# S5 output products of an encoder layer: chunk columns as the stationary operand, two groups side by side, and a transpose behind them

## The chip, the core and the metric

The kernel runs on one core of a Trainium2 chip, as one launch. The metric is the device time of one execution in microseconds (us). Engines are named as in the profile: PE is TensorE's matmul, PEld its weight load, DVE VectorE, ACT ScalarE, POOL GpSimd, SP SyncE, which issues most of the DMAs.

## The reference

One layer of an encoder on 512 tokens of width 1024 in float32: an S5 state-space mixer and a gated MLP mixer in parallel, merged by gates, then cross-attention to 256 memory tokens and a SwiGLU network of width 2816. The change lies in the S5 branch:

```python
def s5_branch(xa, lam_re, lam_im, log_step, b_re, b_im, c_re, c_im, d, w_glu):
    u = xa.reshape(bsz, seq, 32, 16).transpose(1, 0, 2, 3)       # 32 groups of 16 channels
    y = d.reshape(32, 16) * u
    for direction, reverse in ((0, False), (1, True)):
        y = y + s5_scan(u, ..., reverse)      # 64 complex states a group: h_t = lam h_(t-1) + B u_t; y_t = Re(C h_t)
    y = gelu(y.transpose(1, 0, 2, 3).reshape(bsz, seq, 512))
    return y * sigmoid(y @ w_glu)
```

The result is multiplied by `w_proj_a`, gated, and added to the other mixer's.

## The kernel before

Most of the time goes into large products with weights streamed from HBM in blocks of 512 KB. Each float32 operand is split into a rounded part and a rest (`split`: a cast on ACT, line 85, and a subtraction on DVE, line 86; `whi` and `wlo` for weights), and three matmuls make one product (`mm3`; `product`, line 1103, for the blocks that follow the Strassen pattern with seven block products). `next_w` hands out the split weight blocks and keeps loads and splits running ahead.

The S5 branch runs beside these products as a generator, `s5_program`. `tick(us)` is called after each block of matmuls; it advances a planned clock, in units of 5.2 us, runs what `later(n, fn)` has put off by n units, and lets the generator go on. The order that results is the program order; the framework then schedules the instructions of each engine by a simulated time line, and `in_order` (`keep_in_program_order`) holds marked instructions in program order. Each engine runs its own list in order.

The 512 positions are cut into 64 chunks of 8 (`NCH` = 64, `Q` = 8), the 32 groups into four octets (`NO` = 4, `GO` = 8 groups). For octet `o`:

- `s5_kernels(o)` builds `e0` and `e1` (how a chunk's start state reaches its 8 outputs) on DVE, then in `products` the short convolution kernel `pk`, with 32-column strips of the array at `tile_position=(0, 32 * j)`. `store` copies it into `ks`, a tile with the tag `y`. That tag has one buffer, shared with the results. `spill` writes `ks` to HBM (`kd`), `load` reads it back as the Toeplitz matrices `tt` (one buffer, on POOL's queue for octets 0 and 1, on SP's for 2 and 3).
- `s5_inputs(o)` makes each chunk's input to the states, `s5_scan` carries the states over the chunks on DVE (`zh`).
- `s5_outputs(o)` copies the states at the chunk starts into `ss` (two buffers, lines 918 and 919), and `mix_` multiplies: for each group three matmuls with a 128-column weight (`tt`, `e0`, `e1`) and 64 moving columns (`u`, `ss`), so `py` has (position in chunk, channel) on its 128 partitions and (group, chunk) along the rows. `emit` applies gelu into `y` and stores it with eight DMAs, alternately on SP and POOL, to `yd[o]` in HBM.

Octets 0 and 1 have their kernels built early; those of 2 and 3 are built after the outputs of 0 and 1. All this stands beside the end of the gate products (`gb_evac`, line 1140, a sigmoid) and the products with `w_proj_b` (banks `bx`, `bq`, `qv`; `kept`, line 1130, copies a bank into `u`). When they are done, `ygt` reads `yd` back (line 1224), and the product with `w_glu` follows.

Of the kernel before, what the change touches and what calls it, by code (L numbers as in the profile page):

```python
# [9 lines left out]
F32 = mybir.dt.float32  # L10
F32R = mybir.dt.float32r
AF = mybir.ActivationFunctionType
# [5 lines left out]
P = 128  # L18
# [9 lines left out]
C = 16  # L28
# [11 lines left out]
Q = 8  # L40
NCH = T // Q
NO = 4
GO = G // NO
# [9 lines left out]
def hybrid_layer_kernel(  # L53
# [8 lines left out]
    nc = tc.nc  # L62
# [14 lines left out]
    def bank(name):  # L77
        return pm.tile([P, 512], F32, tag="mm", name=name)

    def aux(name, shape=(P, 512)):  # L80
        return pa.tile(list(shape), F32, tag="aux", name=name)
# [11 lines left out]
    in_order = tc.keep_in_program_order  # L93
# [349 lines left out]
    def later(n, fn):  # L443

        side["later"].append((side["now"] + n, fn))
# [30 lines left out]
    ident = cp.tile([P, P], F32, name="ident")  # L476
# [25 lines left out]
    def row_sums(src):  # L502
        ss = np_.tile([P, 2], F32, tag="ss", name="ss", bufs=2)
        for i in range(2):
            sum_sq(ss[:, i:i + 1], src[:, HALF[i]])
        return ss
# [31 lines left out]
    def slot(tag, shape, dt, name, place=NEAR):  # L538
        n = math.prod(shape[1:])
        t = sp.tile([P, KD * T + ROOM[tag]], dt, tag=tag, name=name)[:, place[tag]:place[tag] + n]  # L540
        return t.rearrange("p (a b c) -> p a b c", a=shape[1], b=shape[2]) if len(shape) == 4 else (
            t.rearrange("p (a b) -> p a b", a=shape[1]))
# [6 lines left out]
    s5p = s5.enter_context(tc.tile_pool(name="s5", bufs=1))  # L549
# [47 lines left out]
    ss = row_sums(xt[:, 1, :])  # L597
    for t in range(1, NT):
        rms_scale(xt[:, t, :], g_mix, xt[:, t, :], ss)
        if t == 1:  # L600
            ss = row_sums(xt[:, 2, :])
# [4 lines left out]
        if t == 2:  # L606
            ss = ss3
# [7 lines left out]
    yd = [dp.tile([GO * C, Q, NCH], F32, name=f"yd{o}") for o in range(NO)]  # L615
# [159 lines left out]
    def lc(t, g):  # L775
        return t[:, g].rearrange("p a b -> p (a b)")
# [129 lines left out]
    def s5_outputs(o):  # L906
        gs = slice(o * GO, (o + 1) * GO)
        while ("oct", o) not in st:
            yield None
        e_re, e_im, tt = st["oct", o]  # L910
        zh, u = st["zh"], st["u"]
        ss = s5p.tile([P, 2, GO, NCH], F32, tag="wt", name="ss", bufs=2)
        ss = (ss[:, 0], ss[:, 1])
        for i, s in enumerate(ss):
            zv = zh[:, :, i, gs].rearrange("p n g -> p g n")
            nc.gpsimd.memset(s[lo_, :, 0:1], 0.0)
            nc.gpsimd.memset(s[hi_, :, NCH - 1:NCH], 0.0)
            nc.scalar.copy(s[lo_, :, 1:NCH], zv[lo_, :, 0:NCH - 1])
            nc.scalar.copy(s[hi_, :, 0:NCH - 1], zv[hi_, :, 0:NCH - 1][:, :, ::-1])

        def mix_():
            ps = aux("py", (P, GO, NCH))
            for g in range(GO):
                nc.tensor.matmul(ps[:, g, :], tt[:, g, :], u[:, o * GO + g, :], start=True, stop=False)
                nc.tensor.matmul(ps[:, g, :], lc(e_re, g), ss[0][:, g, :], start=False, stop=False)
                nc.tensor.matmul(ps[:, g, :], lc(e_im, g), ss[1][:, g, :], start=False, stop=True)
            later(1, lambda: emit(ps))

        def emit(ps):
            y = s5p.tile([P, GO, NCH], F32, tag="y", name="y")  # L930
            nc.scalar.activation(y, ps, AF.Gelu_apprx_tanh)
            ydo = yd[o].rearrange("(g c) l n -> l c g n", c=C)
            for l in range(Q):
                (nc.sync, nc.gpsimd)[l % 2].dma_start(ydo[l], y[C * l:C * l + C])

        later(0.5, mix_)
        yield 0.1

# [48 lines left out]
    u = s5p.tile([P, G, NCH], F32, tag="u", name="u")  # L987
# [74 lines left out]
    for h in range(H):  # L1062
        ps = bank("psv")
# [56 lines left out]
    def unit_bank(name):  # L1120
        return bank(name).rearrange("p (j t) -> p j t", j=2)
# [45 lines left out]
    for q, ts in ((5, T1), (6, T0)):  # L1167
        for i in range(2):
            k = slice(2 * i, 2 * i + 2)
# [95 lines left out]
    h = slot("A", (P, NT, D), F32, "h")  # L1265
# [223 lines left out]
    for t0 in (0, 2):  # L1489
        ps = {t: bank(f"pt{t - t0}") for t in (t0, t0 + 1)}  # L1490
# [21 lines left out]
    def acts(unit, f):  # L1512

        if unit < 4:
            return (a_up, a_lo_)[f][:, 2 * unit:2 * unit + 2, :]
        if not rest:
            rest.append(fp.tile([P, KD, T], F32, tag="full", name="rest", bufs=1))
        return rest[0][:, 2 * f:2 * f + 2, :]
# [36 lines left out]
    def put(u, f, ts, src):  # L1555
        dst = acts(u[1] // 512, f)[:, :, ts]
        if u[0] is w_gate:
            nc.scalar.activation(dst, src, AF.Silu)
        else:
            nc.vector.tensor_tensor(dst, dst, src, ALU.mult)  # L1560
# [7 lines left out]
    ps = [bank("pf0"), bank("pf1")]  # L1568
# [67 lines left out]
    for i, u in enumerate(UNITS):  # L1636
        final = i == len(UNITS) - 1
        x, v = begun
        q = unit_bank("pq")
# [132 lines left out]
    for i in range(2):  # L1772
        p = aux("pcut", (P, 256))
# [37 lines left out]
```

## Time and profile before

| what | value |
|---|---|
| median of three runs | 889.34 us |
| lowest, highest | 888.95, 893.28 us |
| the profiled execution | 889.93 us |
| its span in the profile | 888.2 us |
| granted TensorE clock, mean | 0.996 |
| products `py`, first to last | 247.0 to 306.9 us |
| matmul records of `py` | 192 (three lines of 64) |

The span is what the profile covers, from the first instruction to the last; the profiled execution's own time has 1.7 us more. A matmul of full float32 operands shows up as two records. In a timeline row a bracket tells the engine's idle time before the instruction and what ended it; `x2` at the end counts merged instructions. Rows of the chain of waits give the start, the length, and what the chain ran through.

### The profile page before, as it was taken

To read this page: it belongs to the slowest core of one execution; us is meant where nothing else is said; L and a number is where in the kernel's file an instruction comes from. 1 tells how busy PE (TensorE), PEld (TensorE's weight loads), DVE (VectorE), ACT (ScalarE), POOL (GpSimd) and SP (SyncE) were. 2 spreads that over 40 slices of the span, in tenths; PEclk is the share of its full clock that TensorE was granted. 3 is DMA by queue.
4 is the path that set the end of the run, shared out by engine and by line. 5 is a ranking of instruction groups with operands and counts; after the bars stand their busy time and mean duration, and the time that the engine had idled before them with its cause. 6 is when DMAs were issued, how large, how long until landed. Compare 5 with 4: busy or idle time off the path is not lost.

```text
span 888.2 us, 14796 instructions
## 1 busy us (share of the span) xinstructions
PE 870.7 (98%) x5744; PEld 776.9 (87%) x5744; DVE 643.3 (72%) x1048; ACT 486.2 (55%) x714; POOL 106.8 (12%) x165
## 2 busy tenths in 40 slices
PE   8999999999999999999999999999999999999996
PEld 5788888888888988889899978999999999988875
DVE  6698644899757367659857736776878767899875
ACT  5745975244396253448556625645455454655664
POOL 1005201111032101000001001101120111000010
PEclk9999999999999999999999999999999999999999
DMA  8669367887425699734579736637899998356572
GB/s 255 198 185 227 75 190 168 212 190 190 124 79 155 177 323 233 257 111 148 184 217 253 196 95 189 167 109 170 215 241 225 216 237 228 95 176 214 192 239 93
DMA packets 118408, 165.36 MB, mean 186 GB/s; under 512 B 11825, under 2 KB 84161, under 8 KB 118210
## 3 DMA queue, kind: packets, MB, share of 16 engines
q1 hardware_dynamic: 97474, 135.74, 47.1%
q0 software_dynamic: 20576, 28.15, 20.1%
q8 instruction: 45, 0.74, 0.3%
q10 hardware_dynamic: 288, 0.52, 0.2%
q14 instruction: 25, 0.20, 0.1%
HBM read 157.61 MB, written 46.63 MB: 230 GB/s over the span
## 4 chain that ended last, share of the span: by engine, by line
PE 89%; DMA 3%; DVE 2%; ACT 2%; SPq 2%; issue 1%; POOL 0%; POOLq 0%; DVEq 0%; ACTq 0%
PE pf L358 25%; PE pt L358 17%; PE px L1112 12%; PE pq L1112 6%; PE dx L358 5%; PE dq L358 3%; PE pv L1112 3%; PE qx L1112 2%; PE dv L358 2%; PE pz L873 2%; PE psc L358 1%; PE qq L1112 1%; PE ptr L520 1%; PE po L358 1%; PE bq L1112 1%; DMA slab<-in_s_log_step_dram 1%
## 5 line engine op out<-in xcount | busy, mean ns | idle before, releaser
L86 DVE TENSOR_TENSOR wlo<-wraw,whi 128x1024 fp32r<-128x1024 f32 (+1 forms) x145 | 172.3, 1188 | 92.8 <-ACT whi L85 92.4
L85 ACT CAST whi<-wraw 128x1024 fp32r<-128x1024 f32 (+1 forms) x145 | 148.5, 1025 | 150.6 <-PE pf L358 41.7
L358 PE MATMUL pf<-xn,whi 128*128 128x512 f32 x448 | 139.3, 391 | 0.0
L358 PEld LDWEIGHTS pf<-xn,whi 128*128 128x128 f32 x448 | 83.5, 188 | 16.8
L358 PE MATMUL pf<-xn,wlo 128*128 128x512 f32 x224 | 87.3, 390 | 0.0
L1112 PE MATMUL px<-fn,whi 128*128 128x256 f32 x480 | 83.3, 276 | 0.0
L1112 PEld LDWEIGHTS px<-fn,whi 128*128 128x128 f32 x480 | 72.6, 188 | 0.2
L85 ACT CAST whi<-b 128x1024 fp32r<-128x1024 f32 x40 | 42.2, 1054 | 50.7 <-PE px L1112 27.7
L86 DVE TENSOR_TENSOR wlo<-b,whi 128x1024 fp32r<-128x1024 f32 x40 | 48.9, 1223 | 28.0 <-ACT whi L85 28.0
L1112 PE MATMUL px<-fn,wlo 128*128 128x256 f32 x240 | 66.4, 277 | 0.0
L1112 PE MATMUL pq<-s,whi 128*128 128x256 f32 x320 | 55.0, 276 | 0.0
L358 PE MATMUL dx<-whi,s 128*128 128x512 f32 x170 | 53.4, 391 | 0.4 <-DVE h L1736 0.4
L85 ACT CAST whi<-t 128x1024 fp32r<-128x1024 f32 x30 | 31.6, 1054 | 35.3 <-PE pv L1112 12.4
L86 DVE TENSOR_TENSOR wlo<-t,whi 128x1024 fp32r<-128x1024 f32 x30 | 36.7, 1225 | 19.4 <-ACT whi L85 19.4
L358 PEld LDWEIGHTS pf<-xn,wlo 128*128 128x128 f32 x224 | 42.0, 188 | 8.8
L1112 PEld LDWEIGHTS pq<-s,whi 128*128 128x128 f32 x320 | 48.2, 188 | 0.0
L1112 PEld LDWEIGHTS px<-fn,wlo 128*128 128x128 f32 x240 | 45.1, 188 | 0.0
L358 PE MATMUL pt<-whi,xn 128*128 128x512 f32 x128 | 43.5, 409 | 1.2 <-ACT xn L85 1.2
L1112 PE MATMUL pq<-s,wlo 128*128 128x256 f32 x160 | 44.2, 276 | 0.0
L358 PEld LDWEIGHTS dx<-whi,s 128*128 128x128 f32 x170 | 31.8, 188 | 7.5 <-issue 0.8
L358 PE MATMUL dx<-wlo,s 128*128 128x512 f32 x85 | 33.1, 391 | 0.2 <-DVE wlo L86 0.2
L275 POOL DMA_DIRECT2D dsum<-in_w_down_dram x12 | 13.3, 1109 | 163.3 <-DMA dsum<-in_w_down_dram 163.2
(453 smaller groups left out, 2264.7 us busy)
## 6 DMA issues: line engine op xcount, KB each, us to landing
wraw<-in_w_in_dram SPq DMA_DIRECT2D x36, 512.0 KB, 4.7
dsum<-in_w_down_dram SPq DMA_DIRECT2D x20, 512.0 KB, 5.7
wraw<-dsum SPq DMA_DIRECT2D x20, 512.0 KB, 4.0
b<-in_w_gate_dram SPq DMA_DIRECT2D x15, 512.0 KB, 6.8
b<-in_w_up_dram SPq DMA_DIRECT2D x15, 512.0 KB, 5.1
wraw<-in_w_down_dram SPq DMA_DIRECT2D x15, 512.0 KB, 4.0
dsum<-in_w_down_dram POOLq DMA_DIRECT2D x10, 512.0 KB, 7.4
dsum<-dsum POOLq DMA_DIRECT2D x10, 512.0 KB, 8.3
```

What stands on the lines that cost most here:

```text
L85: hi = nc.scalar.copy(dst_hi, src)
L86: lo = nc.vector.tensor_tensor(dst_lo, src, dst_hi.bitcast(F32), ALU.subtract)
L275: plan[j + step][1].append((0, lambda d=dst, x=more: nc.gpsimd.dma_start(d, x, accum_op=ALU.add)))
L358: m = nc.tensor.matmul(ps, a[x], b[y], start=start and i == 0, stop=stop and i == 2, skip_group_check=free)
L520: nc.tensor.transpose(ps[:, j, :], src[:, k * P:(k + 1) * P], ident)
L873: nc.tensor.matmul(ps[:, g, :], wt[:, g, :], u[:, o * GO + g, :], start=True, stop=True)
L1112: nc.tensor.matmul(ps[:, j, :], a[x], b[y], start=start and j == k == i == 0, stop=k == 3 and i == 2, skip_group_check=True)
```

## The change

`mix_` swaps the operands: the 64 chunk columns of `u` or `ss` are now the weight, and the 128 columns of `tt`, `e0` or `e1` are moving. Two groups, `h` and `4 + h`, are put on two column halves of the array, and their matmuls alternate. `py` so has (group half, chunk) on the partitions and (position, group, channel) along the rows. `emit` only copies it to `y`; a new step `turn_y` transposes it in four full 128 x 128 pieces back to (position half, group, channel) on the partitions, and another new step `put` applies gelu, writes over `y`, and stores it with two DMAs. The steps are half a unit apart. Matmuls and transposes are marked `in_order`, which the former matmuls were not.

```diff
         def mix_():
-            ps = aux("py", (P, GO, NCH))
-            for g in range(GO):
-                nc.tensor.matmul(ps[:, g, :], tt[:, g, :], u[:, o * GO + g, :], start=True, stop=False)
-                nc.tensor.matmul(ps[:, g, :], lc(e_re, g), ss[0][:, g, :], start=False, stop=False)
-                nc.tensor.matmul(ps[:, g, :], lc(e_im, g), ss[1][:, g, :], start=False, stop=True)
+            ps = aux("py", (P, 4, 2, 4, C))
+            for h in range(4):
+                for k in range(3):
+                    for j in range(2):
+                        g = 4 * j + h
+                        a = u[:, o * GO + g, :] if k == 0 else ss[k - 1][:, g, :]
+                        b = (tt[:, g, :], lc(e_re, g), lc(e_im, g))[k]
+                        in_order(nc.tensor.matmul(ps[64 * j:64 * j + 64, :, :, h, :].rearrange("p q d c -> p d q c"), a,
+                                                  b.rearrange("p (d q c) -> p d q c", d=2, q=4),
+                                                  start=k == 0, stop=k == 2, tile_position=(0, 64 * j)))
             later(1, lambda: emit(ps))
 
         def emit(ps):
-            y = s5p.tile([P, GO, NCH], F32, tag="y", name="y")
-            nc.scalar.activation(y, ps, AF.Gelu_apprx_tanh)
-            ydo = yd[o].rearrange("(g c) l n -> l c g n", c=C)
-            for l in range(Q):
-                (nc.sync, nc.gpsimd)[l % 2].dma_start(ydo[l], y[C * l:C * l + C])
+
+            y = s5p.tile([P, 512], F32, tag="y", name="y")
+            nc.scalar.copy(y, ps.rearrange("p q d g c -> p (q d g c)"))
+            later(0.5, lambda: turn_y(y))
+
+        def turn_y(y):
+            ps = aux("pyt", (P, 2, 4, NCH))
+            for q in range(4):
+                in_order(nc.tensor.transpose(ps[:, :, q, :], y[:, q * P:(q + 1) * P], ident))
+            later(0.5, lambda: put(y, ps))
+
+        def put(y, ps):
+            nc.scalar.activation(y, ps.rearrange("p s q n -> p (s q n)"), AF.Gelu_apprx_tanh)
+            ydo = yd[o].rearrange("(s f) (d q) n -> d f s (q n)", s=2, d=2)
+            for d in range(2):
+                (nc.sync, nc.gpsimd)[d].dma_start(ydo[d], y[64 * d:64 * d + 64].rearrange("p (s r) -> p s r", s=2))
```

## The prediction

> **What bounds the kernel now.** The page first: over the whole span TensorE is the limit, and the chain that ended last is mostly its matmuls.
>
> ```profile
> span 888.2 us, 14796 instructions
> PE 870.7 (98%) x5744; PEld 776.9 (87%) x5744; DVE 643.3 (72%) x1048; ACT 486.2 (55%) x714; POOL 106.8 (12%) x165
> PE 89%; DMA 3%; DVE 2%; ACT 2%; SPq 2%; issue 1%; POOL 0%; POOLq 0%; DVEq 0%; ACTq 0%
> ```
>
> Averages hide the stage of the edit, so next I cut its stretch (the four products `py` run between 247 and 307 us) into windows; columns are the window's length and the busy time of PE, PEld, DVE, ACT, POOL.
>
> ```profile
> 244.00:255.00 11.00, 11.00 (x74) 9.93 (x73) 3.46 (x4) 10.69 (x11) 2.19 (x5) 1.00 0.21 71
> 255.00:265.00 10.00, 8.87 (x113) 7.78 (x115) 6.89 (x9) 9.92 (x14) 4.50 (x12) 1.00 0.42 98
> 265.00:280.00 15.00, 14.77 (x150) 14.20 (x140) 13.93 (x17) 11.72 (x16) 3.43 (x11) 1.00 0.43 129
> 280.00:300.00 20.00, 18.87 (x209) 18.54 (x209) 9.92 (x11) 7.64 (x11) 5.78 (x12) 1.00 0.62 170
> ```
>
> So PE is nearly full, but ACT is full with it up to 265 and DVE from 265 to 280. TensorE work taken out here is worth its time only where the other engine gives way too. The timeline of PE shows the waits in it (bracketed: idle before, and what ended it):
>
> ```profile
> 260.62 0.38 PE L1112 MATMUL bq<-s,whi 128*128 128x256 f32 x1 [0.78 <-ACT s L85]
> 261.34 0.38 PE L1112 MATMUL bq<-s,whi 128*128 128x256 f32 x1 [0.34 <-DVE s L86]
> 280.76 0.38 PE L1112 MATMUL bx<-yb_hi,whi 128*128 128x256 f32 x1 [0.99 <-ACT u L1130]
> 301.40 0.41 PE L924 MATMUL py<-u,tt 128*128 128x64 f32 x2 [1.20 <-DMA tt<-kd]
> 306.75 0.48 PE L1112 MATMUL bq<-s,whi 128*128 128x256 f32 x2
> 317.25 2.83 PE bq L1112 x24
> ```
>
> PE waits for ACT, for ACT again, and last for the kernel matrix `tt` of octet 3. The rows at 301.40 and 306.75 also price the old form: 24 matmuls of an octet in 5.35 us. The last row is from the chain of waits: one `product` of 24 matmuls, 2.83 us; from 306.75 to its end at 320.08 the chain holds PE rows alone.
>
> **The change, part by part. TensorE.** Removed: 4 x 5.35 = 21.4 us. Added: 24 matmuls an octet with 64-column weights in two column halves and 128 moving columns, and four transposes. No row shows a 64-column half. The nearest rows are the `pk` matmuls, four 32-column strips with 128 moving columns, issued with the strip as the inner loop as the new ones are, and the transposes `pw`, which use the whole array (from the chain in order of time):
>
> ```profile
> 283.46 0.28 PE L1112 MATMUL bx<-yb_lo,whi 128*128 128x256 f32 x1
> 283.58 0.28 PE L1112 MATMUL bx<-yb_hi,wlo 128*128 128x256 f32 x1
> 283.79 0.42 PE L814 MATMUL pk<-e,bd 128*32 128x128 f32 x8
> 284.03 0.27 PE L819 MATMUL pk<-e,bd 128*16 128x16 f32 x16
> 284.13 0.62 PE L814 MATMUL pk<-e,bd 128*32 128x128 f32 x16
> 284.57 0.28 PE L819 MATMUL pk<-e,bd 128*16 128x16 f32 x16
> 284.78 0.38 PE L1112 MATMUL qv<-yb_hi,whi 128*128 128x256 f32 x1
> 77.97 0.87 PE pw L866 x8
> ```
>
> A matmul has two records. Sixteen strip records take 284.57 - 284.13 = 0.44 us, 0.11 for each set of four side by side; a `pw` record alone takes 0.87 / 8 = 0.109. So a set of 128 moving columns costs 0.11 however many strips share it. Twelve pairs of two records: 24 x 0.11 = 2.64 us if the halves overlap, 48 x 0.11 = 5.28 if they don't. I take 2.64, since four strips overlap. Entering the strips costs 283.79 - 283.58 = 0.21 where the usual step is 0.12, and leaving 0.21 after a set that took 0.10 before: 0.2 together. Four transposes are the `pw` row, 0.87. New sum 2.64 + 0.20 + 0.87 = 3.71, a saving of 1.64 an octet, 6.6 in all, as a ceiling from PE alone. The matmuls alone end 5.35 - 2.84 = 2.5 earlier.
>
> The Trainium skill (TensorEngine Tiling (Array Packing), Key Properties) says that changing the tiling mode drains TensorE, which speaks against eight more changes here. The trace agrees: the 0.2 us just read. By the rule alone the sum has eight more drains without a price; by the row they are 0.8 us, already in it.
>
> **ACT, octet 0.** The removed gelu `L931` and what follows it, on ACT:
>
> ```profile
> 250.46 1.04 ACT L85 CAST whi<-wraw 128x1024 fp32r<-128x1024 f32 x1
> 251.52 1.28 ACT L931 ACT_TABLE_LOAD   x1
> 252.99 0.60 ACT L931 ACTIVATE y<-py 128x512 f32<-128x512 f32 x1 [0.19 <-PE py L926]
> 253.49 1.11 ACT L918 COPY ss<-zh 64x504 f32<-64x504 f32 x1
> ...
> 258.03 1.28 ACT L1140 ACT_TABLE_LOAD   x1
> 259.32 0.60 ACT L1140 ACTIVATE part<-pf 128x512 f32<-128x512 f32 x1
> 259.94 2.18 ACT L85 CAST s<-zf 128x512 fp32r<-128x512 f32 x4
> 260.60 1.29 DVE L86 TENSOR_TENSOR s<-zf,s 128x512 fp32r<-128x512 f32 x2 [3.07 <-ACT s L85]
> ```
>
> The four `ss` copies of octet 2 wait for a buffer that `py` of octet 0 reads, then the table goes back to sigmoid, and only then come the casts `s` for which DVE (3.07 us idle) and PE wait. In the new form `emit` is a plain copy, and the gelu moves behind the last sigmoid in program order (`put` comes one unit, 5.2 us of planned TensorE work, after `emit`, and the sigmoids follow the last feature block). The load at 258.03 goes, and the one at 251.52 moves behind the casts. New order: `py` ends at 252.97 - 2.5 = 250.5, the cast at 251.5, copy 0.6 to 252.1, `ss` 258.03 - 253.49 = 4.54 to 256.6, sigmoid 0.6, first `s` done at 257.8 instead of 260.57: 2.8 earlier. PE gets there at 260.62 - 0.78 - 2.5 + 0.87 (transposes) = 258.2, so the gain at `bq` is 2.3 to 2.8; I take 2.5. The added copy is priced by the `wt` copy, which has its shape:
>
> ```profile
> L867 ACT COPY wt<-pw x16: 561/588/604, 79.0 to 135.8; 128x512 f32<-128x512 f32 x16
> ```
>
> **Octets 1 and 2.** From 265 to 280 DVE is busy 13.93 of 15 us; it begins this queue with the row at 260.60, so it moves forward by the same 2.5 and hardly more. What PE saves on octet 1 it waits for DVE again. A further piece: the 0.99 us before 280.76, where ACT copied `u` late because a table load and the gelu of octet 1 stood ahead. I take 1.0, with bounds 0 and 2. Octet 2 is bound otherwise, by the way of octet 3's kernel matrix:
>
> ```profile
> 285.00 0.38 ACT L829 COPY ks<-pk 128x256 f32<-128x256 f32 x1 [0.52 <-PE pk L819]
> 287.70 6.54 DMA kd<-ks
> 294.37 5.12 SPq L845 DMA_DIRECT2D tt<-kd  x8
> 298.25 2.28 DMA tt<-kd
> ```
>
> Its spill, load and landings are serial from 285.00 to 301.4 and untouched by the edit. The 1.64 of octet 2 ends as a longer wait at 301.40: nothing.
>
> **Octet 3.** After `py` PE runs on without a wait to 320.08, so 1.64 lies on the path.
>
> **Stores.** Eight stores of 32 KB an octet become two of 128 KB; four issues on SP become one, and on POOL too:
>
> ```profile
> 279.32 1.75 SPq L934 DMA_DIRECT2D yd<-y  x4
> 281.11 3.11 SPq L845 DMA_DIRECT2D tt<-kd  x5
> DMA to landing us min/median/max: 1.7/2.1/4.0
> 307.03 0.60 ACT L931 ACTIVATE y<-py 128x512 f32<-128x512 f32 x1 [6.40 <-PE py L926]
> 314.71 1.77 SPq L1224 DMA_DIRECT2D ygt<-yd  x4
> ```
>
> Shorter queues for `tt` of octet 2 (1.75 to about 0.45): octet 2 isn't on the path by the above, so nothing. Larger stores may land from 1.7 to 4.0 us. The last result now passes two more steps, about two products, 5.7 us, with 0.87 of transposes; before, 314.71 - 307.63 = 7.1 us lay between gelu and reload. That cover just holds; I add 0.3, and up to 2.5 if `glu` must wait.
>
> Sum: -2.5 - 1.0 - 0 - 1.64 + 0.3 = -4.8. Against the profiled execution (889.93 us, 1.7 outside its span) 885.1; it lies 0.6 above the median of the three times, 889.34, so I forecast 884.5. The bounds: at best -2.8 - 2.0 - 1.64 - 1.64 (octet 2 counts too) = -8.1, at worst -2.3 - 0 - 1.64 + 2.5 = -1.4; so 881.2 to 887.9.
>
> **Rivals.** (a) PE stays the only bound: all 6.6, and the 1.1 us of waits for `s` go: 881.6. For it: PE 98%; against it: the DVE window. (b) The gain is swallowed: DVE's queue keeps its times, `tt` of octet 3 comes at 301.4 as before, and only octet 3's 1.64 remains: 887.7. For it: the serial chain; against it: DVE's 3.07 us of idle time before `s`. The Trainium skill (TensorEngine Tiling (Array Packing), PSUM Bottleneck) warns of this case: tiling speeds TensorE, not the emptying of PSUM. The ACT windows before 265 agree with it; the copy of 0.6 us that comes in against the 1.28 us load that goes out does not. (c) Slower: the one buffer `y`, shared with `ks`, is held through copy, transposes, gelu and store. Place: `ks` of octet 3 needs it at 285.00. If PE takes the transposes of octet 1 only at 283.6, gelu ends at about 284.6, issue and landing add 2.6, and `ks` is 2.2 late. Then `y` of octet 2, copied when `kd` has landed (294.25), gets its gelu after a product, 294.25 + 0.6 + 2.8 + 0.87 + 0.6 = 299.1; if its store stands on SP ahead of the eight `tt` loads, these start at 299.7 for 294.37, 5.3 late. -4.8 + 1.0 + 2.2 + 5.3 = +3.7: 893.0 (bounds +1.5 to +7). It decides if the store goes ahead of L845. Before, octet 1's store did stand among the `tt` loads, octet 2's behind them. (d) The halves don't overlap, or writing `py` in runs of 16 elements is slow: 5.28 + 0.2 + 0.87 - 5.35 = +1.0 an octet, +4 to +5: 893.8. Against it: the `pk` rows.
>
> **How the numbers follow.** A change of some 0.5% (4.4 us) is about what a measurement of this kernel can tell from no change. Forecast 0.42 (0.26 faster beyond that bound, 0.16 within), (a) 0.18 faster, (b) 0.10 within, (c) 0.20 (half slower, half within), (d) 0.10 slower. Faster 0.44, same 0.36, slower 0.20. The range runs from 880.5, below (a), to 894.0, through (c) and (d); outside lie the far ends of (a), (c) and (d), under 2 in 10. The forecast's own is 881.2 to 887.9.
>
> **What would show it.** Right: 24 new matmuls of an octet from first to last in about 2.7 us; no table load between `ss` copies and the last sigmoids; the first `s` cast near 257; `py` of octet 3 near 298 after a wait of some us. Wrong: that product over 5 us; `ks` waiting for `yd`; SP's store ahead of the last `tt` loads; a wait of several us at `glu`.

## The result, and the profile after

The changed kernel takes 904.67 us (median of 4 runs, 903.75 to 905.06); the kernel before, run beside it, 891.15 us (4 runs, 888.95 to 893.28). The ratio is 1.015, 95% interval 1.0117 to 1.0184: slower by 1.5%, above the forecast (884.5) and above the range (to 894.0). The profiled execution took 905.0 us, of which the page covers 903.2.

The page of the changed kernel, its span, the engines and the chain that ended last by engine:

```profile
span 903.2 us, 14797 instructions
PE 867.9 (96%) x5760; PEld 771.5 (85%) x5760; DVE 643.8 (71%) x1048; ACT 486.0 (54%) x716; POOL 102.2 (11%) x153
PE 88%; DMA 5%; ACT 3%; issue 2%; DVE 1%; SPq 1%; POOLq 0%; POOL 0%; ACTq 0%; DVEq 0%
```

PE has 2.8 us less work (870.7 to 867.9) and the span is 15.0 us longer: PE waits more, and the share of DMA in the chain went from 3% to 5%. The same stretches as before, and one more, from the windows of the changed kernel (columns: length; busy time of PE, PEld, DVE, ACT, POOL; granted clock; DMA share; GB/s):

```profile
255.00:265.00 10.00, 9.66 (x154) 8.62 (x153) 9.77 (x12) 8.27 (x15) 0.74 (x4) 1.00 0.23 69
265.00:280.00 15.00, 8.14 (x61) 7.64 (x61) 13.29 (x16) 11.22 (x13) 2.86 (x9) 0.84 0.43 131
280.00:300.00 20.00, 20.00 (x242) 19.50 (x242) 8.57 (x11) 8.27 (x11) 2.80 (x6) 0.95 0.63 196
318.00:335.00 17.00, 1.50 (x11) 1.30 (x10) 3.09 (x5) 2.13 (x3) 3.19 (x4) 0.65 0.96 271
```

Up to 265 PE is fuller than before (9.66 for 8.87). From 265 to 280 it is busy 8.14 us where it was 14.77, at a clock of 0.84. From 318 to 335 it stands nearly still (1.50 us of work, for 15.78 before). What PE waited for between 244 and 342, from the list of waits (total, times, longest):

```profile
PE pf L358 <- ACT yg_hi L85: 15.5, 1, 15.5
PE bx L1128 <- ACT whi L85: 3.7, 1, 3.7
PE bx L1128 <- ACT u L1146: 3.1, 1, 3.1
PE py L929 <- DMA tt<-kd: 2.2, 1, 2.2
```

Before, no wait of PE in this stretch was above 1.2 us. First the edit itself and the first two waits, on the timeline of PE:

```profile
262.07 0.44 PE L929 MATMUL py<-tt,u 128*64 128x128 f32 x4
264.85 0.66 PE L943 MATMUL pyt<-ident,y 128*128 128x128 f32 x4
265.26 0.48 PE L1128 MATMUL bq<-s,whi 128*128 128x256 f32 x2
275.24 0.58 PE L1128 MATMUL bx<-yb_hi,whi 128*128 128x256 f32 x1 [3.73 <-ACT whi L85]
279.16 0.58 PE L1128 MATMUL bx<-yb_hi,whi 128*128 128x256 f32 x1 [3.12 <-ACT u L1146]
```

Octet 1's 24 matmuls take 264.85 - 262.07 = 2.78 us, for 5.35 before; four transposes take 0.41. The two waits follow. ACT shows what PE waited for:

```profile
257.10 2.19 ACT L85 CAST s<-zf 128x512 fp32r<-128x512 f32 x4
...
272.36 1.28 ACT L947 ACT_TABLE_LOAD   x1
273.66 0.60 ACT L947 ACTIVATE y<-pyt 128x512 f32<-128x512 f32 x1
274.15 1.99 ACT L85 CAST whi<-wraw 128x1024 fp32r<-128x1024 f32 x2
277.30 0.37 ACT L829 COPY ks<-pk 128x256 f32<-128x256 f32 x1 [1.17 <-DMA yd<-y]
278.52 0.59 ACT L1146 COPY u<-bx 128x512 f32<-128x512 f32 x1
287.37 0.59 ACT L937 COPY y<-py 128x512 f32<-128x512 f32 x1
290.97 0.60 ACT L947 ACTIVATE y<-pyt 128x512 f32<-128x512 f32 x1 [1.26 <-PE pyt L943]
295.58 0.37 ACT L829 COPY ks<-pk 128x256 f32<-128x256 f32 x1 [1.06 <-DMA yd<-y]
```

The row at 273.66 is octet 0's gelu; it ran at 252.99 before. `whi` stands behind it and its table load, and ahead of these, from 267.15 to 271.7, behind the four `ss` copies of octet 3. Octet 0 holds the one buffer `y` from its copy at 251.43 until its store lands; `ks` of octet 2 waits for that at 277.30, and `u`, which PE waits for, stands behind it on ACT. Then, once the spill of `ks` has landed, octet 1 may have the buffer: it is copied only at 287.37 though its product was ready at 264.85, its gelu runs at 290.97, and `ks` of octet 3 gets it at 295.58. Before, that copy ran at 285.00. From there the serial chain of spill, load and product moves with it: `py` of octet 3 starts at 310.12 instead of 301.40.

Last, the wait at `glu`. The lists of POOL, first of the kernel before, then of the changed one:

```profile
307.92 2.09 POOL L934 DMA_DIRECT2D yd<-y  x4 [10.13 <-ACT y L931]
...
327.39 1.20 POOL L275 DMA_DIRECT2D qsum<-in_w_q_dram  x1 [14.88 <-DMA qsum<-qsum]
```

```profile
305.27 0.61 POOL L950 DMA_DIRECT2D yd<-y  x1 [6.81 <-ACT y L947]
318.68 1.22 POOL L275 DMA_DIRECT2D qsum<-in_w_q_dram  x1 [12.81 <-DMA qsum<-qsum]
319.35 1.18 POOL L950 DMA_DIRECT2D yd<-y  x1
329.84 0.14 POOL L130 MEMSET pad<- 128x48 f32 x1 [9.31 <-DMA yd<-y]
```

`qsum` is a sum of weight blocks for a later stage: SP copies one block of 512 KB, and POOL adds another to it by an accumulating DMA. It stood 19.5 us behind the last store; now it stands right ahead of it. In program order the store still comes first (experiment 1, which holds the two in that order, has it first); the framework issues the accumulate ahead of it. That it does so because its time line has the last gelu later than before is likely, but not shown. The first copy, on SP, went out earlier too: at 311.11, ahead of the last store, where before it stood at 318.41, behind the reload. The chain of the changed kernel runs through both, and through the reload:

```profile
311.11 6.99 DMA qsum<-qsum
319.35 10.21 DMA yd<-y
330.59 3.12 DMA ygt<-yd
334.58 10.59 PE pf L358 x34
```

SP's half of the last store goes out at 317.40. POOL's half has to wait until the accumulate ahead of it has its copy and is issued; it goes out at 319.35 and lands after 10.21 us. Over all DMAs of `yd` in this kernel the shortest time to landing is 2.5 and the median 3.6 us. So `ygt` is issued at 329.7, and PE, done with the products at about 319.1, starts `glu` at 334.58. Before, it started at 319.91. These 14.7 us are nearly the whole 15.0; up to the end of the products the changed kernel is still 1.0 us ahead (their last matmul starts at 318.81, for 319.79).

### The profile page after: what moved, and what is told of

Its sections match the earlier page's. It is cut to its first block, busy times and chain, and to the rows that moved or that the text cites. A ratio compares the mean times of both kernels' runs of the same rounds, so it can differ in the third digit from the quotient of the medians.

```text
span 903.2 us, 14797 instructions
## 1 busy us (share of the span) xinstructions
PE 867.9 (96%) x5760; PEld 771.5 (85%) x5760; DVE 643.8 (71%) x1048; ACT 486.0 (54%) x716; POOL 102.2 (11%) x153
## 4 chain that ended last, share of the span: by engine, by line
PE 88%; DMA 5%; ACT 3%; issue 2%; DVE 1%; SPq 1%; POOLq 0%; POOL 0%; ACTq 0%; DVEq 0%
PE pf L358 25%; PE pt L358 17%; PE px L1128 12%; PE pq L1128 6%; PE dx L358 5%; PE dq L358 3%; PE pv L1128 3%; PE qx L1128 2%; PE bx L1128 2%; PE dv L358 2%; PE pz L873 2%; DMA yd<-y 1%; PE psc L358 1%; PE qq L1128 1%; PE ptr L520 1%
```

## The experiments

Theory: two things put the last reload late. **(A)** The place on POOL's queue: the last store is issued directly behind the accumulating DMA. **(B)** The buffer `y`, shared with `ks`, is held from the copy to the landing of the store, and everything behind it (`u`, `ks` of octets 2 and 3, `py`, the last gelu) slides. Rivals: the swapped product is itself slow; the late gelu of octet 0 is the harm, not the buffer; the POOL order is harmless. Ratios are to runs of the kernel before on the same chip, beside each group of experiments; they are not quotients of the medians given, and can differ from these by some tenths of a percent.

**1. The order on POOL put back.**

```diff
-            plan[j + step][1].append((0, lambda d=dst, x=more: nc.gpsimd.dma_start(d, x, accum_op=ALU.add)))
+            plan[j + step][1].append((0, lambda d=dst, x=more: onto(d, x)))   # onto: in_order for qsum[4, 0]
...
+            if o == NO - 1:
+                in_order(put_)          # POOL's store of octet 3
```

> The changed kernel, with one order fixed: on POOL's list octet 3's store stands ahead of the accumulating 512 KB DMA (qsum) that was pulled in front of it. Theory 1 (the last store is late because of that DMA): the store lands in about 3.5 us instead of 10.2 and is issued 2 us earlier, ygt is read near 321 instead of 329.7, TensorE's wait at the glu product falls from 15.5 to about 7.5 us; 896.5 us. Rival (the two added steps make the result late by themselves, whatever the queue): the wait stays over 12 us; 902 to 905 us.

Measured: 899.38 us (896.07 to 905.23), ratio 1.0081 (1.0049 to 1.0113); span 897.4. From its chain and its waits:

```profile
318.91 2.92 DMA yd<-y
322.01 5.08 DMA ygt<-yd
```

```profile
PE pf L364 <- ACT yg_hi L85: 7.6, 1, 7.6
```

The store now lands after 2.92 us instead of 10.21 and the wait at `glu` halves, from 15.5 to 7.6. (A) is worth about 5 us here (by the two ratios, 1.015 and 1.0081, about 6), but the kernel is still slower than before: the last gelu itself is late (318.03, for 307.03 before), and the two waits near 275 are untouched (3.9 and 3.1 us).

**2. The results in a buffer of their own.** `y` takes the tag `rb`, a buffer that a tile of the setup (`raw_b`) no longer needs; `ks` keeps the tag `y` to itself.

```diff
-            y = s5p.tile([P, 512], F32, tag="y", name="y")
+            y = s5p.tile([P, 512], F32, tag="rb", name="y")
```

> The changed kernel with a buffer of its own for y (the space of a tile that is dead by then), so that ks no longer waits for y's store; with it the last store comes ahead of the qsum DMA on POOL too. Theory 1 (shared buffer and queue together make the loss): the two waits of TensorE between 271 and 279 us go (6.8 us, and some 2 us at a slow clock), tt of octet 3 comes some 8 us earlier, the wait at glu mostly goes; 886 to 889 us. Rival (lateness of the added steps): the wait at glu stays; 893 to 896 us.

Measured: 885.98 us (885.03 to 887.73), ratio 0.9922 (0.9885 to 0.9959); span 884.3. In the order that results, the store goes ahead of the accumulate by itself (308.64 and 327.44), so this run mends (A) too; against experiment 1, which has (A) mended, the edit differs in the buffer and the marks of order alone, and the medians stand 13.4 us apart. Its waits and, from ACT's timeline, the two `ks` copies:

```profile
PE bx L1128 <- ACT whi L85: 3.9, 1, 3.9
PE pyt L943 <- ACT y L937: 1.9, 1, 1.9
```

```profile
262.91 0.37 ACT L829 COPY ks<-pk 128x256 f32<-128x256 f32 x1
287.14 0.37 ACT L829 COPY ks<-pk 128x256 f32<-128x256 f32 x1 [0.47 <-PE pk L819]
```

`ks` of octet 2 runs 14.4 us earlier than in the changed kernel, that of octet 3 8.4 us, neither waits for `yd`, and the wait at `glu` is gone (its start: 317.38). The wait for `whi` is as long as in experiment 1, so it isn't the buffer's. (B) is shown, and with it that the swap is no loss.

**3. The swapped product alone.** Gelu straight from `py`; the transposes are left out, so the stored result is in another order.

```diff
-            nc.scalar.copy(y, ps.rearrange("p q d g c -> p (q d g c)"))
-            later(0.5, lambda: turn_y(y))
...
+            nc.scalar.activation(y, ps.rearrange("p q d g c -> p (q d g c)"), AF.Gelu_apprx_tanh)
```

> The swapped products and the two larger stores, but gelu straight from the product as before and no transposes (they are left out, so the stored result is in another order). Theory 1 (the swap itself frees TensorE, and the loss comes from the added steps): faster than the old kernel by 5 to 8 us, 882 to 885 us. Rival (what TensorE saves is swallowed by DVE and by the serial way of tt): 888 to 890 us.

Measured: 886.53 us (885.74 to 888.3), ratio 0.9938 (0.9912 to 0.9964). The buffer is still shared, but held for one step only. The rival that the swapped product is slow falls.

**4. The kernel before with its gelu planned later** (`later(2, ...)` for `later(1, ...)` ahead of `emit`).

> The old kernel, with gelu and stores of each octet put off by one more unit, the delay that the added steps bring, and nothing else. Theory 1: y is held longer, but the store still comes ahead of qsum on POOL, so little is lost; 890 to 893 us. Rival (lateness alone is the cost): 897 to 903 us.

Measured: 889.94 us (888.11 to 896.38), ratio 0.9988 (0.9957 to 1.0018). Inconclusive: octet 0's gelu ran at 253.37, as before, since the framework orders each engine by its simulated time line, not by the plan alone. So this run didn't make the gelu late, and says nothing on what a late gelu costs.

**5. The kernel before with the accumulate ahead of the last store.** Plan place 43 for the first copy, and octet 3's POOL stores planned two units later.

```diff
-              [(51 + 2 * i, 2) for i in range(4)] + [(85 + 3 * i, 3) for i in range(3)] +
+              [(43, 3)] + [(51 + 2 * i, 2) for i in range(1, 4)] + [(85 + 3 * i, 3) for i in range(3)] +
```

> The old kernel, with only the order on POOL's list turned round at one place: the accumulating 512 KB DMA (qsum) ahead of POOL's half of octet 3's stores (its SP copy is issued eight weight blocks earlier for that). Theory 1 (a store behind that DMA lands late): POOL's stores of octet 3 land 5 to 10 us later, past the old 314.7 us of the reload, and TensorE waits at the glu product; 893 to 898 us. Rival (the order is harmless, the swap's own lateness did it): 889 to 891 us.

Measured: 897.9 us (897.67 to 906.98), ratio 1.0101 (1.0059 to 1.0143); span 896.1. POOL's timeline and the chain of this run:

```profile
312.47 1.20 POOL L275 DMA_DIRECT2D qsum<-in_w_q_dram  x1 [15.98 <-DMA qsum<-qsum]
313.13 2.65 POOL L944 DMA_DIRECT2D yd<-y  x4
```

```profile
314.70 8.36 DMA yd<-y
323.33 4.16 DMA ygt<-yd
```

With the old product and the old use of the buffer PE waits 9.5 us at `glu`. The place costs twice: POOL, which stands 15.98 us until the accumulate's copy has landed, issues the stores at 313.13 for 307.92 before, and the last of them lands only after 8.36 us. (A) alone makes this kernel 1% slower; nothing of the swap is needed for it.

**6. Two result buffers.** As experiment 2, with two halves of `rb` taken in turn by the octets (`y = st["yy"][:, o % 2]`).

> As with a buffer of its own for y, but two of them in turn (the dead tile's two halves), so that a copy never waits for the store of the octet before. Theory 1: TensorE's 1.9 us before the transposes of octet 1 go, the 3.9 us behind ACT's list stay; 884 to 885 us. Rival (that wait is covered by the other): 886 us, no change against one buffer.

Measured: 883.92 us (883.07 to 884.92), ratio 0.9923 (0.99 to 0.9946); span 883.0. `glu` starts at 316.28. It beats both kernels; from experiment 2 the ratio can't tell it.

**7. The steps run at once** in the changed kernel, buffer shared: `turn_y(y)` and `put(y, ps)` called directly, not put off by half a unit.

> The changed kernel with the two added half units taken out of the plan: transposes and gelu follow the copy at once in program order, the buffer stays shared with ks. Theory 1 (the half units let the store slip behind the qsum DMA and let gelu of octet 0 slip to 273 us, the buffer passes this on): both waits shrink, since gelu of octet 0 comes near 262; 886 to 889 us. Rival (the shared buffer costs by itself): ks of octet 3 still waits for the store of octet 1, 891 to 896 us.

Measured: 889.84 us (887.91 to 892.79), ratio 0.9998 (0.9974 to 1.0022); span 887.3. From ACT's timeline:

```profile
261.63 1.28 ACT L947 ACT_TABLE_LOAD   x1
262.92 0.60 ACT L947 ACTIVATE y<-pyt 128x512 f32<-128x512 f32 x1
266.71 0.37 ACT L829 COPY ks<-pk 128x256 f32<-128x256 f32 x1 [0.62 <-DMA yd<-y]
```

Against the changed kernel octet 0's gelu runs 10.7 us earlier and `ks` of octet 2 10.6 us earlier, and the last store (309.83) stands ahead of the accumulate again. Without the two half units the whole loss is gone; but nothing is gained.

**8. Both: steps at once and an own buffer.**

> Both: y in a buffer of its own, and no half units between copy, transposes and gelu. Theory 1: with gelu of octet 0 ahead of the ss copies on ACT, the weight cast that TensorE waited for (3.9 us) comes in time; 881 to 884 us. Rival (TensorE's savings are swallowed by DVE in any order): 886 us as before.

Measured: 891.36 us (887.5 to 892.46), ratio 0.9999 (0.9969 to 1.0029). A miss: my thought that an early gelu helps with any buffer falls. The wait for `whi` is gone, as expected, but `bq` starts at 262.96 (257.77 in the changed kernel, 258.50 in experiment 2), and PE waits 2.0 us for `e` on DVE and 4.6 at `glu`. Against experiment 2 only the steps differ, and that kernel is 5.4 us faster: with a buffer of its own, putting the steps off is better. The early gelu isn't what `bq` waits for: its table load starts at 261.89, when the casts of `s` (258.26) and `whi` (260.84) are done. In this order `pk` of octet 2 stands ahead of `bq` on PE, at 261.40, and it is `pk` that waits for `e`; in experiment 2 `bq` comes first. How much of the 5.4 us that order costs is not shown by a run.

**9. Own buffer, accumulate ahead** (experiment 2 with the plan of experiment 5).

> The changed kernel with `y` in a buffer of its own (as in a2_own_y), and now the accumulate of 512 KB into `qsum` put ahead of the POOL half of octet 3's store again. Theory (two separate causes: the shared buffer, and the place of the last store on POOL's queue): the buffer is mended, so `ks` of octets 2 and 3 does not wait for `yd`, but the reload `ygt` waits for a store that lands 8 to 11 us after its issue: the wait at `glu` for yg_hi is 7 to 12 us, and the time is 885.98 + 7 to 10 = 893 to 896. Rival (one cause: the shared buffer made everything late, and the accumulate did harm only because of that lateness): the store is early enough, no wait over 2 us at `glu`, 885 to 888.

Measured: 889.46 us (886.62 to 891.71), ratio 0.9996 (0.9969 to 1.0023). The POOL list shows that it tested something else:

```profile
295.93 1.25 POOL L275 DMA_DIRECT2D qsum<-in_w_q_dram  x1
313.80 0.64 POOL L955 DMA_DIRECT2D yd<-y  x1 [16.62 <-ACT y L953]
316.90 0.14 POOL L130 MEMSET pad<- 128x48 f32 x1 [2.47 <-PE bq L1138]
```

Its first copy came so much earlier that the accumulate was issued 17.9 us ahead of the store. The reload is issued 3.0 us behind the store, and no wait above 0.5 us remains at `glu`. So an accumulate far ahead on the queue does no harm here; one 0.7 us ahead does (landings of 10.21 and 8.36 us). The rival, that lateness through the buffer is needed, isn't shown by this either: experiment 5 has the harm without it. Why this run is 3.5 us above experiment 2 stays open; `py` of octet 3 starts 3.4 us later, at 304.72.

**10. Octet 3's `ss` copies on POOL**, on experiment 6 with the last store pinned as in experiment 1.

```diff
+            copy = nc.scalar.copy if o < NO - 1 else nc.gpsimd.tensor_copy
```

> The version with two `y` buffers of their own (b2_two_y), the last store pinned ahead of the accumulate, and the four `ss` copies of octet 3 on POOL in place of ACT. Theory (the 3.4 us that PE still waits near 275 for a weight cast come from ACT's queue: four `ss` copies of 4.5 us in all, a cast, a table load of 1.28 and a gelu of 0.6 stand ahead of it): without the four copies the wait falls below 1 us and the time to 880 to 882. Rival (DVE, busy 13.3 of 15 us there, sets that place): the wait moves to a `wlo` or `s` of DVE, and the time stays 882.5 to 885. Second rival: the copies on POOL (no row of these kernels prices them) take so long that `py` of octet 3 waits for `ss`; over 885.

Measured: 890.25 us (888.62 to 891.77), ratio 0.9999 (0.9973 to 1.0024). The waits of PE:

```profile
PE py L936 <- DMA tt<-kd: 5.1, 2, 4.5
PE pf L364 <- ACT yg_hi L85: 3.1, 1, 3.1
```

The wait for `whi` near 275, 3.4 us in experiment 6, is gone: ACT's queue was its cause. The time did not follow. PE waits for `tt` of octet 3 instead, as the chain of spill and load hardly moved, and the last store goes out at 312.13 for 307.77. The four copies take 10.95 us on POOL, for 4.46 on ACT; how much of the loss they are and how much is the other order is not settled.

## Why the prediction was wrong, step by step

**Swapped product: right.** Forecast 2.64 and 0.2 for the mode; measured 2.78, the mode included. The halves overlap; rival (d) is out. The transposes were over-sized: a `pw` row of eight records was read as four transposes, where each transpose is one record: 0.41, not 0.87.

**Octet 0 on ACT: right.** The load ahead of the sigmoids is gone, the first `s` cast starts at 257.10, and `bq` at 257.77 for 260.62, 2.85 us earlier (forecast 2.3 to 2.8). The lower bound had the transposes ahead of `bq`; they came behind octet 1's product.

**Octets 1 and 2: the first step that failed.** I took 1.0 us off because gelu and table load would no longer stand ahead of `u` of octet 1, and priced octet 2 at nothing. The gelu that I moved out of octet 0 has to run somewhere: with its table load it stands at 272.36, behind four `ss` copies and ahead of the cast `whi` (3.7 us of PE wait), and its store holds `ks` of octet 2, with `u` behind it (3.1 us). The wait for `whi` goes when the gelu runs early (experiments 7 and 8) and when the copies leave ACT (experiment 10), which speaks for the two together as its cause. PE had no other work ready in these waits, and its granted clock fell to 0.84. I moved the gelu without asking what is queued behind its new place. At the end of the products 1.0 us was left of the 5.1 forecast to there.

**Rival (c): the right mechanism, at the wrong place and price.** It let octet 1 have the buffer on time and made `ks` of octet 3 2.2 us late; the buffer was already 277.30 - 262.91 = 14.4 us late at `ks` of octet 2 (against experiment 2), and `ks` of octet 3 came 10.6 us late. Its condition was not met (SP issued octet 2's store at 308.66, behind the `tt` loads of 303.80), and the kernel was slower all the same.

**The tail: the largest miss.** I added 0.3 us, at most 2.5, on a cover of 7.1 us. PE waited 15.5. The term counted two steps of delay in program order; the last gelu came 9.8 us later (316.8), 8.7 of them because `py` of octet 3 itself started that much later, which I had held fixed at 301.4; and for the landing I took 1.7 to 4.0 from the old rows, where nothing stood right ahead of the store on POOL. It was 10.21. The accumulate of `qsum` was not in my list of queues at all: I went through SP's `tt` loads, not through POOL's own list.

**The sum itself.** With own buffers, experiment 6, the span falls from 888.2 to 883.0, by 5.2 us, where the sum gave 4.8; not by the same terms, though (a wait of 3.4 for `whi` remains there), so that they lie so near is in part luck; its ratio, 0.9923, says nearer 7 us. That lies between rival (b), 1.6 us faster than before, and rival (a), 7.7; no run here tells what bounds the mended kernel.

## What to carry to other kernels

A step that is taken off a busy place comes back elsewhere: look up what stands behind it on its engine at the new place, and which buffer it keeps longer, before the gain is booked. A buffer's time runs from its first write to the landing of the last DMA that reads it, and a shared tag makes another stage pay for it. Before a reload that ends a stage, read the issuing queue's whole list, other work's DMAs included, as a small store directly behind a large transfer took on its time here.

## What the runs showed of the chip

A store of 128 KB issued on POOL 0.7 us behind an accumulating DMA of 512 KB landed after 10.21 us (changed kernel), four of 32 KB in the same place after up to 9.4 us (experiment 5); without it ahead, one of 128 KB landed after 2.92 us (experiment 1). The accumulate itself landed 10.4 us after its issue in the changed kernel and 9.9 in experiment 5, so about 329.1 and 322.4; the last store behind it was there at 329.56 and 323.06, about half a microsecond later. That the DMA engines were full then (a share of 0.96 from 318 to 335) doesn't explain it alone: a load of 512 KB that SP issued at 318.70 landed after 5.1 us. The Trainium skill (DMA: Bandwidth & Descriptors, Two DMAs through the same engine are not ordered) says that within one queue of one DMA engine descriptors start in order; the rows agree, as far as a store that starts behind a large transfer lands late.

After a long wait PE was slow for a while. At `glu` of the changed kernel, on PE's timeline:

```profile
336.88 0.63 PE L358 MATMUL pf<-yg_hi,wlo 128*128 128x512 f32 x1
337.31 0.63 PE L358 MATMUL pf<-yg_hi,whi 128*128 128x512 f32 x1
341.13 0.39 PE L358 MATMUL pf<-yg_hi,wlo 128*128 128x512 f32 x1
341.36 0.40 PE L358 MATMUL pf<-yg_hi,whi 128*128 128x512 f32 x1
```

The step is 0.43 us until about 339.9, 5.3 us after the start, with a granted clock of 0.50, and 0.23 then. So the wait cost more than its length: from the start of `glu` to that of the next product it took 13.6 us, for 12.2 before, and these 12.2 hold a wait of 1.1 us (for `ya_hi`) that is gone in the changed kernel; about 2.5 us go to the slow clock. The windows show the same for the waits near 275, by their clock of 0.84. The Trainium skill (TensorE: Matmul & The Clock Gate, What's actually happening) has half the clock after at least one stretch of about 3.4 us of idling and the full one after at least one such stretch of work; the halving agrees, and the way back took 5.3 us here, more than one stretch.
